# Ten weight slots of the adaptive conditioning move from beside the routers into the mixers, between products and heads

## The chip, the cores and the metric

One Trainium2 chip, one core. The metric is device time in microseconds for one execution of the whole program.

## The reference, cut to what matters

256 tokens of width 1024, float32, pass through two blocks. Block 1 is a mixer (16 attention heads of 64) followed by a mixture of 32 experts. Block 2 has two layers: a mixer of differential attention and a Fourier part with 16 experts behind it, then a short convolution with 16 experts behind it. In block 2 each layer l modulates its inputs by six vectors that come from a condition:

```python
def ada_params(cond, w_ada, b_ada):
    m = jax.nn.silu(cond) @ w_ada + b_ada
    return jnp.split(m[..., None, :], 6, axis=-1)

def modulate(x, g, shift, scale):
    return rmsnorm_2(x, g) * (1 + scale) + shift

def even_mixer(h, hc, w_in, q_norm, k_norm, lam, subln, w_out, lam_init, cos, sin, ctx_out):
    ...
    q, k, v, f = jnp.split(h @ w_in, cuts, axis=-1)
    q = apply_rope(rmsnorm_2(qk_heads(q), q_norm), cos, sin) * scale
    k = apply_rope(rmsnorm_2(qk_heads(k), k_norm), cos, sin)
    ...
```

In each layer the vectors 0 and 1 shift and scale the mixer's input, 2 gates its output, 3 and 4 shift and scale the experts' input, 5 gates their output.

## The kernel before, in words

**Phases.** The program runs mixer1, moe1, mixer2, moe2(0), mixer3, moe2(1), one behind the other. Each expert phase begins with its router (scores, a mask, positions, the gathering products `xg`) and goes on with one expert after the other (`gu`, then `d`).

**The weight stream.** All large weights come in tiles of 2 MB, 128 partitions by 4096 floats, in one fixed list that `plan` writes down. `Stream` puts each tile into a slot of a ring: six of its own, and up to three rooms (X, Y, Z) that are lent to it in stretches where nothing else needs them. Slots are reused in the order in which they were filled, and only when the kernel has called `done` for the tile that is in them. The loads (line 236) are all issued by SyncE's queue in the order of the list, and each issue waits for the last reader of the slot, so that one issue that waits holds up all behind it.

**The adaptive units.** There are twelve, named (l, v). `ada_unit` (line 569) takes two weight tiles, its two slots. For each it runs 8 small matmuls `ada_ps` (the trace counts 16), copies the result from PSUM into a row on ScalarE, and calls `done`. Then 8 transposes `adaT_ps` turn the row into columns, and VectorE reduces them.

**Where the units stand before.** (0,0) and (0,1) in mixer1; (0,3) and (0,2) in moe1's router, as fills between its steps; (0,4) at the start of mixer2; (1,0) and (1,1) between mixer2's products by way of `merged`, one slot behind each product; (0,5) and (1,2) in the router of moe2(0); (1,3) and (1,4) in mixer3; (1,5) in the router of moe2(1).

**Mixer2's products.** Five products of the normed input with 512 columns each, named by their first column (768, 0, 512, 1280, 1792), have eight k-steps: a weight tile's slice is split into a high part `wh` on ScalarE (line 338) and a low part `wl` on VectorE (line 339), and TensorE runs four matmuls with `wh` and two with `wl` (the function `three`). Behind the first four products `post` norms the heads and turns them (rope): `hss` on VectorE, `rs_r` on GpSimd, `xn` and `ro` on VectorE and GpSimd, for one half of the tokens and then the other; at last the transposes `qk_ps` (line 1328) on TensorE. The first two products have 8 heads of queries or keys, the next two 4, the last none. `chain` advances a product, the transposes of the one before, the norm, and then the fill. The compiler's scheduler may move independent instructions past each other, so the order on an engine is read from the built program.

**Mixer1's end.** `flow` interleaves the attention of eight pairs of heads (`duo`) with four output products (`out`), which read the tiles `out1`.

Of the kernel before, what the change touches and what calls it, by code (L numbers as in the profile page):

```python
# [10 lines left out]
F32 = mybir.dt.float32  # L11
I32 = mybir.dt.int32
F32R = mybir.dt.float32r
# [140 lines left out]
def chain(units, fill=iter(()), last=iter(())):  # L154
# [11 lines left out]
        last = finish  # L166
    for _ in last:
        pass


def merged(a, b):

    next(a)
    yield
    next(a)
    yield
    next(a, None)
    next(b)
    yield
    next(b)  # L180
    yield
    next(b, None)
    yield


def row_of(*units):
# [63 lines left out]
class Net:  # L250
# [180 lines left out]
    def plan(self):  # L431
        I, add = self.I, self.st.add

        def ada(l, v, hfs=(0, 1)):
            src = I["ada_w_2"][l].rearrange("(p k) f -> p k f", k=8)
            for hf in hfs:
                f0 = v * 1024 + hf * 512
                add(("ada", l, v, hf), src[:, :, f0:f0 + 512])

        def out(name, w):  # L440
            w = w.rearrange("(k p) d -> p k d", p=128)
            for i in range(2):
                add((name, i), w[:, 4 * i:4 * i + 4, :])

        win = I["w_in"][0].rearrange("(p k) f -> p k f", k=8)

        def in1(col):
            w = win[:, :, col:col + 512]
            add(("in1", col), *((w[:, 0:4], w[:, 4:8]) if col == 512 else (w,)))

        in1(512)
        in1(0)
        ada(0, 0, (0,))
        in1(1024)
        ada(0, 0, (1,))
        in1(2048)
        ada(0, 1, (0,))
        in1(1536)
        ada(0, 1, (1,))
        in1(2560)  # L460
        out("out1", I["w_out"][0])
        ada(0, 3)
        ada(0, 2)
        win2 = I["attn_w_in_2"][0].rearrange("(p k) f -> p k f", k=8)
        for e in range(32):
            add(("g", 0, e), I["w_gate"][0, e].rearrange("(p k) f -> p k f", k=8))
            add(("u", 0, e), I["w_up"][0, e].rearrange("(p k) f -> p k f", k=8))
            add(("d", 0, e), I["w_down"][0, e].rearrange("(n p c) d -> p n c d", n=2, c=2))
            i = CTX.index(e) // 2 - 1 if e in CTX and CTX.index(e) % 2 == 0 else -1
            if i >= 0:  # L470
                add(("ctx", i), win2[:, :, 768 + 512 * i:1280 + 512 * i])
        ada(0, 4)
        for i, c0 in enumerate((768, 0, 512, 1280, 1792)):
            if c0 == 512:
                add(("in2", 512), win2[:, :, 512:768], win2[:, :, 2304:2560])
            else:
                add(("in2", c0), win2[:, :, c0:c0 + 512])
            if i < 4:
                ada(1, i // 2, (i % 2,))
        out("out2", I["attn_w_out_2"][0])  # L480
        ada(0, 5)
        ada(1, 2)
        self.plan_moe2(0)
        win3 = I["conv_w_in_2"][0].rearrange("(p k) f -> p k f", k=8)
        for q in range(2):
            for n in (1, 2, 0):
                f0 = n * 1024 + q * 512
                add(("in3", n, q), win3[:, :, f0:f0 + 512])
            ada(1, 3 + q)
        out("out3", I["conv_w_out_2"][0])  # L490
        ada(1, 5)
        self.plan_moe2(1)

    def plan_moe2(self, l):
# [151 lines left out]
    def mixer1(self):  # L646
        nc, tc, I = self.nc, self.tc, self.I
        with ExitStack() as cx:
# [251 lines left out]
            self.lend("X", ("g", 0, CTX[0]))  # L900
            w = self.P("wr1", "p (k e) -> p k e", k=8)
            nc.gpsimd.tensor_tensor(w, w, self.P("g_ffn")[:, :, None].to_broadcast([128, 8, 64]), op=ALU.mult)
            flow([duo(4, 2), out(0, 0, 1), duo(5, 2), duo(6, 2), out(0, 1, 1), duo(7, 2), out(1, 0, 1, 1)])
            for _ in out(1, 1, 4):
                pass

# [171 lines left out]
    def moe1(self):  # L1078
        nc, tc, sm = self.nc, self.tc, self.sm
        with ExitStack() as cx:  # L1080
# [8 lines left out]
            for c in range(2):  # L1089
                nc.vector.scalar_tensor_tensor(zz[:, c, :], z[:, c, 0:36], r[:, c:c + 1], self.kp[:, a:a + 36], op0=ALU.mult,  # L1090
                                               op1=ALU.add)
            ze, zg = zz[:, :, 0:32], zz[:, :, 32:36]

            fills = [self.ada_unit(0, v, wk, ps, "a", "a", 3, 0, 3, wk.tile([128, 1024], F32, tag="row", name="row", bufs=2))
                     for v in (3, 2)]
            for i in (0, 0, 1):
                next(fills[i])
            mg = sm.tile([128, 2], F32, name="mg")
            nc.vector.tensor_reduce(out=mg, in_=zg, axis=AX.X, op=ALU.max)
            ohg = self.first_hot(wk, zg, mg, 4, "g")  # L1100
# [14 lines left out]
            mask = wk.tile([128, 2, 32], BF16, name="mask", bufs=1)  # L1115
            nc.vector.tensor_tensor(mask, oh1, oh2, op=ALU.add)
            pos = self.prefix(ps, mask, 32)
            next(fills[1])
            nc.vector.tensor_tensor(m2, m2, m1, op=ALU.subtract)
            nc.scalar.activation(m2, m2, AF.Exp)  # L1120
            g1 = sm.tile([128, 2], F32, name="g1")
# [18 lines left out]
                        (lambda n, c, j: wd[:, 2 * n + c, j * 256:j * 256 + 256]), done)  # L1140

            def first():
                for f in fills:
                    next(f, None)

                self.over = sm.tile([128, 2, 32], F32, name="over", bufs=1)
                nc.vector.tensor_scalar(self.over, pos[:, 0:2, :], 31.5, None, op0=ALU.is_ge)
                nc.vector.tensor_tensor(self.over, self.over, comb, op=ALU.mult)
                most = sm.tile([128, 1], F32, name="most", bufs=1)
                nc.vector.tensor_reduce(out=most, in_=pos[:, 2, :], axis=AX.X, op=ALU.max)  # L1150
                self.most = sm.tile([128, 1], I32, name="most_i", bufs=1)
                nc.vector.tensor_copy(self.most, most)
# [128 lines left out]
    def mixer2(self):  # L1281
        nc, tc, I, sm = self.nc, self.tc, self.I, self.sm
        with ExitStack() as cx:
# [116 lines left out]


            room, lows = [], {}
            high = self.cp.tile([128, 2, 8, 128], F32R, tag="xh", name="high")
            part = lambda k, c: (high[:, c, k, :], lows[k // 4][c][:, k % 4, :])

            def f_at(c):
# [2 lines left out]
            def sums():  # L1409
                fs = wk.tile([128, 2, 256], F32, tag="ro", name="fs", bufs=2)  # L1410
                for s, op in enumerate((ALU.add, ALU.subtract)):
                    nc.vector.tensor_tensor(fs[:, s, :], f_at(0), f_at(1), op=op)
                return fs

            tabs = self.roomy[:, 3072:3584]
            nc.gpsimd.dma_start(tabs, I["k_c"])
            chain([pair(768, 8, 1, 0), pair(0, 8, 0, 0), pair(512, 4, 0, 4, f_at),
                   pair(1280, 4, 1, 4, lambda c: v[:, c, 0:256]),
                   pair(1792, 0, 0, 0, lambda c: v[:, c, 256:768])],
                  merged(*(self.ada_unit(1, i, wk, ps, "pj", "tp", 4, 0, 2, q2[:, 2048:3072]) for i in range(2))))  # L1420
            fs = sums()
            t = self.room("X").rearrange("p (i b) -> p i b", b=512)
            room.extend((t[:, 0:4], t[:, 4:8]))
# [33 lines left out]
    def mixer3(self):  # L1457
        nc, tc = self.nc, self.tc
        with ExitStack() as cx:
# [11 lines left out]
            for q in range(2):  # L1471
# [22 lines left out]
                if q:  # L1494
                    self.lend("X")
                st.done(*[("in3", n, q) for n in (1, 2, 0)])
                for _ in self.ada_unit(1, 3 + q, wk, ps, "pj", "tp", 5, 0, 2, row):
                    pass
            self.router_bias(1, wk, "cv_a", 2, ps, "tp", 2)
            w = [st.take(("out3", i), 4) for i in range(2)]  # L1500
            for hf in range(2):
# [8 lines left out]
    def moe2(self, l):  # L1510
        nc, tc, sm = self.nc, self.tc, self.sm
        with ExitStack() as cx:
# [7 lines left out]
            aff = wk.tile([128, 2, 16], F32, name="aff", bufs=1)  # L1520
            for c in range(2):
                nc.vector.scalar_tensor_tensor(aff[:, c, :], z[:, c, 0:16], r[:, c:c + 1], self.rbias, op0=ALU.mult, op1=ALU.add)

            def unit(*u):
                row = wk.tile([128, 1024], F32, tag="row", name="row", bufs=2)
                return self.ada_unit(*u, wk, ps, "a", "a", 3, 0, 3, row)

            fill, also = unit(l, 5), iter(()) if l else unit(1, 2)
            next(fill)
            mx = sm.tile([128, 2], F32, name="ec_m")  # L1530
            nc.vector.tensor_reduce(out=mx, in_=aff, axis=AX.X, op=ALU.max)
            nc.vector.tensor_tensor(aff, aff, mx[:, :, None].to_broadcast([128, 2, 16]), op=ALU.subtract)
# [4 lines left out]
            b = ps.tile([16, 2, 128], F32, tag="a", name="affT_ps", bufs=3)  # L1537
            for c in range(2):
                nc.tensor.transpose(b[:, c, :], aff[:, c, :], self.ident)
            next(fill)  # L1540
            next(also, None)
            aT = wk.tile([16, 256], F32, tag="WT", name="affT")
            bT = b.rearrange("p c t -> p (c t)")
            m8 = None
# [14 lines left out]
            nc.vector.tensor_tensor(ge[:, :, 0:16], aff, tb, op=ALU.is_gt)  # L1559
            nc.vector.tensor_tensor(ge[:, :, 16:32], aff, tb, op=ALU.is_equal)  # L1560
            pre = self.prefix(ps, ge, 32)
            next(also, None)
            need = wk.tile([128, 16], F32, name="need", bufs=1)
            nc.vector.tensor_scalar(need, pre[:, 2, 0:16], -1.0, 32.0, op0=ALU.mult, op1=ALU.add)
            nb = need[:, None, :].to_broadcast([128, 2, 16])
# [21 lines left out]
            gate = wk.tile([128, 256], F32, name="gate", bufs=1)  # L1587

            def first():
                next(fill, None)  # L1590
                next(also, None)
                self.gate_quarters(l, 5, gate, wk, ps, "a", 3)

            def hook(e):
# [54 lines left out]
```

## Time and profile before

| | us |
|---|---|
| median of 3 runs | 1912.75 (1911.39 to 1913.34) |
| the profiled execution, its own time | 1912.47 |
| its span, first to last instruction | 1910.4 |
| outside the span | 2.1 |

The granted TensorE clock is 0.862 of full speed as a mean over the span. The profiled execution is 0.28 us below the median, so sums made on it apply to the median as they are. TensorE is busy for 71% of the span, VectorE 26%, ScalarE 19%, GpSimd 8%. Of the time of the 16 DMA engines 89.5% goes to the one queue that SyncE feeds.

### The profile page before, as it was taken

What the parts mean: (1) busy time and instruction counts of PE and PEld (TensorE: products, weight loads), DVE (VectorE), ACT (ScalarE), POOL (GpSimd) and SP (SyncE); (2) the same over time, 40 slices, a digit from 0 to 9 for tenths busy, and PEclk for the clock granted to TensorE, in tenths of its full rate; (3) what the DMA queues carried; (4) which work ended last, traced back from release to release, by engine and by line L of the source; (5) the groups of instructions that cost most, each with busy time, mean ns of one, the idle gap of its engine ahead of it and who ended that gap; (6) DMA issues with size and microseconds to landing.
All of it is one profiled execution on the core that took longest, in us unless ns stands there. A gap on an engine that the chain in (4) does not pass through costs nothing.

```text
span 1910.4 us, 27412 instructions
## 1 busy us (share of the span) xinstructions
PE 1363.1 (71%) x11863; PEld 756.5 (40%) x11863; DVE 492.5 (26%) x1189; ACT 361.1 (19%) x786; POOL 158.1 (8%) x217
## 2 busy tenths in 40 slices
PE   6989866667778678998565574565997664654745
PEld 4766533344444346564221221222984231221312
DVE  3666311121111056753010110102664110101101
ACT  4545100010111043742000000001442000000000
POOL 3132000010000034111000000001001000000000
PEclk9999988889999889989787787877998877877868
DMA  9645999999999997248999999999758999999998
GB/s 368 221 173 211 425 428 429 428 428 396 386 421 426 427 406 258 77 176 374 430 430 431 431 430 431 429 431 417 298 227 371 430 431 430 431 430 430 431 430 340
DMA packets 97691, 716.15 MB, mean 375 GB/s; under 512 B 5664, under 2 KB 7840, under 8 KB 56480
## 3 DMA queue, kind: packets, MB, share of 16 engines
q1 hardware_dynamic: 96960, 712.72, 89.5%
q8 instruction: 94, 1.54, 0.3%
q0 software_dynamic: 464, 1.57, 0.2%
q14 instruction: 29, 0.24, 0.0%
q10 hardware_dynamic: 144, 0.08, 0.0%
HBM read 713.30 MB, written 1.05 MB: 374 GB/s over the span
## 4 chain that ended last, share of the span: by engine, by line
DMA 39%; PE 31%; DVE 3%; POOL 2%; ACT 1%; issue 1%; SPq 0%; DVEq 0%; POOLq 0%; ACTq 0%
DMA w<-in_moe_w_up 18%; DMA w<-in_moe_w_gate 12%; PE gu_ps L997 9%; DMA w<-in_moe_w_down 7%; PE cv_ps L364 4%; PE pj_ps L364 3%; PE d_ps L1026 3%; DMA w<-in_w_up 2%; PE cx_ps L1261 2%; PE xg_ps L983 1%; PE sc_ps L1344 1%; PE o_ps L364 1%; PE ada_ps L580 1%; POOL rs_r L299 1%; PE y L1038 1%
## 5 line engine op out<-in xcount | busy, mean ns | idle before, releaser
L997 PE MATMUL gu_ps<-w,xgT 128*32 128x256 f32 (+1 forms) x4096 | 434.8, 586 | 302.4 <-DMA w<-in_moe_w_up 249.3
L997 PEld LDWEIGHTS gu_ps<-w,xgT 128*32 128x32 f32 x4096 | 146.4, 129 | 568.7 <-issue 262.9
L1005 DVE TENSOR_TENSOR h<-gu_ps,hs 64x256 f32<-64x256 f32 (+1 forms) x64 | 46.6, 727 | 778.0 <-ACT hs L1004 778.0
L1026 PE MATMUL d_ps<-w,eh 128*32 128x256 f32 x3072 | 203.1, 414 | 18.1 <-DMA w<-in_moe_w_down 7.2
L1004 ACT ACTIVATE hs<-gu_ps 64x256 f32<-64x256 f32 (+1 forms) x64 | 31.1, 487 | 921.7 <-PE gu_ps L997 921.7
L1026 PEld LDWEIGHTS d_ps<-w,eh 128*32 128x32 f32 x3072 | 97.2, 119 | 103.3 <-issue 30.4
L364 PE MATMUL pj_ps<-wh,roomX 128*128 128x512 f32 x352 | 106.4, 422 | 6.1 <-DVE xn L391 5.1
L339 DVE TENSOR_TENSOR wl<-w,wh 128x512 fp32r<-128x512 f32 x136 | 95.2, 712 | 41.9 <-ACT wh L338 36.5
L338 ACT ACTIVATE wh<-w 128x512 fp32r<-128x512 f32 x136 | 84.5, 630 | 90.3 <-PE cv_ps L364 36.7
L1018 PE MATMUL t_ps<-kp,h 64*128 64x64 f32 x192 | 25.3, 239 | 86.4 <-DVE h L1005 80.2
L364 PEld LDWEIGHTS pj_ps<-wh,roomX 128*128 128x128 f32 x352 | 69.6, 202 | 29.4 <-issue 6.7
L364 PE MATMUL cv_ps<-roomX,wh 128*128 128x256 f32 x384 | 71.9, 289 | 3.8 <-ACT wh L338 3.8
L983 PE MATMUL xg_ps<-Sg,xh 128*128 128x128 f32 x512 | 68.9, 293 | 2.3 <-DVE Sg L976 1.7
L983 PEld LDWEIGHTS xg_ps<-Sg,xh 128*128 128x128 f32 x512 | 63.8, 204 | 12.5 <-issue 10.8
L364 PE MATMUL pj_ps<-wl,roomX 128*128 128x512 f32 x176 | 59.4, 418 | 12.3 <-DVE wl L351 6.8
L1018 PEld LDWEIGHTS t_ps<-kp,h 64*128 64x128 f32 x192 | 16.6, 138 | 127.7 <-DVE h L1005 116.4
L364 PEld LDWEIGHTS cv_ps<-roomX,wh 128*128 128x128 f32 x384 | 61.9, 197 | 5.0 <-ACT wh L338 4.2
L364 PE MATMUL cv_ps<-roomX,wl 128*128 128x256 f32 x192 | 55.5, 289 | 0.2 <-DVE wl L339 0.2
L580 PE MATMUL ada_ps<-w,sc 128*32 128x512 f32 x384 | 48.9, 617 | 2.3 <-DVE x L271 2.2
L1038 PE MATMUL z<-ysb,WT 32*128 32x256 f32 x512 | 36.7, 400 | 16.9 <-DVE ysb L1033 16.9
L299 POOL TENSOR_TENSOR rs_r<-rs_r,mhalf 128x1 f32<-128x1 f32 (+3 forms) x45 | 44.9, 997 | 3.8
L1261 PE MATMUL cx_ps<-w,roomX 128*128 128x512 f32 x96 | 43.6, 602 | 0.0
(394 smaller groups left out, 1451.3 us busy)
## 6 DMA issues: line engine op xcount, KB each, us to landing
w<-in_moe_w_gate SPq DMA_DIRECT2D x64, 2048.0 KB, 38.5
w<-in_moe_w_up SPq DMA_DIRECT2D x64, 2048.0 KB, 28.8
w<-in_moe_w_down SPq DMA_DIRECT2D x63, 2048.0 KB, 32.7
w<-in_w_gate SPq DMA_DIRECT2D x32, 2048.0 KB, 20.3
w<-in_w_up SPq DMA_DIRECT2D x32, 2048.0 KB, 22.7
w<-in_w_down SPq DMA_DIRECT2D x32, 2048.0 KB, 23.5
w<-in_ada_w SPq DMA_DIRECT2D x24, 2048.0 KB, 11.9
w<-in_attn_w_in SPq DMA_DIRECT2D x7, 2048.0 KB, 14.6
```

The source lines that it names most:

```text
L299: nc.gpsimd.tensor_tensor(r, r, self.mhalf.to_broadcast(shape), op=ALU.pow)
L338: return (self.nc.scalar.activation(hi, src, AF.Copy), self.nc.vector.tensor_tensor(lo, src, hi.bitcast(F32), op=ALU.subtract))
L339: self.nc.vector.tensor_tensor(lo, src, hi.bitcast(F32), op=ALU.subtract))
L364: self.nc.tensor.matmul(o, l[a], r[b], start=first and n == 0, stop=last and n == 2)
L580: nc.tensor.matmul(b[32 * j:32 * j + 32, :], self.sc[:, 4 * kk + j, :], w[:, 4 * kk + j, :], start=kk == 0, stop=kk == 1)
L983: nc.tensor.matmul(b[:, k, :], self.xh[:, c, 2 * kq + k, :], Sg[:, c].rearrange("p e s -> p (e s)"), start=c == 0, stop=c == 1)
L997: nc.tensor.matmul(gu[32 * j:32 * j + 32, :], xgT[:, k, sl:sl + 32], w[:, n * Fh:n * Fh + Fh], start=k == 0, stop=k == 7)
L1005: nc.vector.tensor_tensor(h, gu[0:64, :].rearrange("p (m c) -> p c m", c=nch), hs.rearrange("p (m c) -> p c m", c=nch), op=ALU.mult)
L1018: nc.tensor.transpose(ht[:, c * 64:c * 64 + 64], h[:, c, :], self.ident[0:64, 0:64])
L1026: nc.tensor.matmul(d[32 * j:32 * j + 32, :], hT[:, c, n * 32:n * 32 + 32], wd(n, c, j), start=i == 0, stop=i == 2 * nch - 1)
L1038: nc.tensor.matmul(y[j][:, c, :], WT[r, c * 128:c * 128 + 128], ysb[r, :], start=e == 0 and c == 0, stop=e == ne - 1, skip_group_check=True)
L1261: nc.tensor.matmul(b, xr["hT"][:, k, c * 128:c * 128 + 128], w[:, k, :], start=k == 0, stop=k == 7)
```

## The change

Ten slots, that is five units, change place; the work in each and the sum of all transfers stay.

- (0,2) and (0,3) leave moe1's router and stand in mixer1's last `flow`, one behind `duo(5)`, one behind the second half of the first output group. Their order in the plan is swapped.
- `merged` goes. In mixer2 the new `fills` runs a whole unit, two slots, behind each of the first four products: (1,0), (1,1), (0,5), (1,2). The transposes of a unit come with the next fill. The rows lie in two halves of `xh`, so `high`, which has the same buffer, is allocated behind the products.
- (0,5) and (1,2) leave the router of moe2(0). (1,5) leaves the router of moe2(1) and stands in mixer3 directly behind (1,4), ahead of the output product.
- The plan follows: each of mixer2's first four input tiles has two adaptive tiles behind it, the experts' tiles of moe2(0) stand directly behind `out2`, and (1,5) stands ahead of `out3`.

```diff
-def merged(a, b):
-    next(a)
-    yield
...
@@ plan
+        ada(0, 2)
         ada(0, 3)
-        ada(0, 2)
...
             if i < 4:
-                ada(1, i // 2, (i % 2,))
+                ada(*((1, 0), (1, 1), (0, 5), (1, 2))[i])
         out("out2", I["attn_w_out_2"][0])
-        ada(0, 5)
-        ada(1, 2)
         self.plan_moe2(0)
...
+        ada(1, 5)
         out("out3", I["conv_w_out_2"][0])
-        ada(1, 5)
         self.plan_moe2(1)
@@ mixer1
-            flow([duo(4, 2), out(0, 0, 1), duo(5, 2), duo(6, 2), out(0, 1, 1), duo(7, 2), out(1, 0, 1, 1)])
+            flow([duo(4, 2), out(0, 0, 1), duo(5, 2), ada(2, row), duo(6, 2), out(0, 1, 1), ada(3, row), duo(7, 2), out(1, 0, 1, 1)])
@@ moe1, router
-            fills = [self.ada_unit(0, v, wk, ps, "a", "a", 3, 0, 3, wk.tile([128, 1024], F32, tag="row", name="row", bufs=2))
-                     for v in (3, 2)]
-            for i in (0, 0, 1):
-                next(fills[i])
...
@@ mixer2
+            def fills():
+
+                u = iter(())
+                for i, lv in enumerate(((1, 0), (1, 1), (0, 5), (1, 2))):
+                    next(u, None)
+                    u = self.ada_unit(*lv, wk, ps, "pj", "tp", 4, 0, 2, self.xh[:, i % 2].rearrange("p k m -> p (k m)"))
+                    next(u)
+                    next(u)
+                    yield
+                next(u, None)
+                yield
...
-                  merged(*(self.ada_unit(1, i, wk, ps, "pj", "tp", 4, 0, 2, q2[:, 2048:3072]) for i in range(2))))
+                  fills())
+            high = self.cp.tile([128, 2, 8, 128], F32R, tag="xh", name="high")
@@ mixer3
-                for _ in self.ada_unit(1, 3 + q, wk, ps, "pj", "tp", 5, 0, 2, row):
-                    pass
+                for v in ((4, 5) if q else (3,)):
+                    for _ in self.ada_unit(1, v, wk, ps, "pj", "tp", 5, 0, 2, row):
+                        pass
@@ moe2, router
-            fill, also = unit(l, 5), iter(()) if l else unit(1, 2)
-            next(fill)
...
```

What this does to the order on the engines is shown at three places. The first is TensorE near the end of mixer1, in the built program of before (`pj_ps` is an output product, `sc_ps`, `pT_ps` and `av_ps` are the attention):

```order
L803 MATMUL sc_ps<-dkT,dqT 128x128 x2
L824 MATMUL pT_ps<-kp,s 128x128 x6
L364 MATMUL pj_ps<-wh,oTf 128x512 x4
L364 MATMUL pj_ps<-wl,oTf 128x512 x2
L803 MATMUL sc_ps<-dkT,dqT 128x256 x2
L803 MATMUL sc_ps<-dkT,dqT 128x128 x2
L832 MATMUL av_ps<-pT,xh 64x256 x2
```

The same place in the changed program:

```order
L786 MATMUL sc_ps<-dkT,dqT 128x128 x2
L807 MATMUL pT_ps<-kp,s 128x128 x6
L349 MATMUL pj_ps<-wh,oTf 128x512 x4
L349 MATMUL pj_ps<-wl,oTf 128x512 x2
L563 MATMUL ada_ps<-w,sc 32x512 x8
L815 MATMUL av_ps<-pT,xh 64x256 x2
L817 MATMUL av_ps<-pT,xh 64x128 x2
```

One slot of (0,2) stands between an output product's step and the attention. There are four such groups of eight and two groups of eight transposes `adaT_ps` from here to the end of mixer1.

The second place is TensorE in mixer2, before, from the end of the first product (768) into the second:

```order
L364 MATMUL pj_ps<-wl,roomX 128x512 x2
L580 MATMUL ada_ps<-w,sc 32x512 x8
L364 MATMUL pj_ps<-wh,roomX 128x512 x4
L364 MATMUL pj_ps<-wl,roomX 128x512 x2
L364 MATMUL pj_ps<-wh,roomX 128x512 x4
L364 MATMUL pj_ps<-wl,roomX 128x512 x2
L364 MATMUL pj_ps<-wh,roomX 128x512 x4
L1328 MATMUL qk_ps<-kp,xn 128x128 x4
L364 MATMUL pj_ps<-wl,roomX 128x512 x2
```

The rest of the second product follows, and the other four `qk_ps` stand at its end. In the changed program the same place reads:

```order
L349 MATMUL pj_ps<-wl,roomX 128x512 x2
L563 MATMUL ada_ps<-w,sc 32x512 x16
L1303 MATMUL qk_ps<-kp,xn 128x128 x8
L575 MATMUL adaT_ps<-kp,xh 128x128 x6
L349 MATMUL pj_ps<-wh,roomX 128x512 x4
L349 MATMUL pj_ps<-wl,roomX 128x512 x2
```

Both slots of the unit and all eight head transposes of the product now stand ahead of the next product's first matmul. Behind the second, third and fourth product it is the same (eight `qk_ps`, then twice four).

The third place is ScalarE at the same point of mixer2 (`ro` is the square for the norm, `qT` the old row of the unit). Before:

```order
L382 ACTIVATE ro<-pj_ps 128x512
L338 ACTIVATE wh<-w 128x512 x2
L269 ACTIVATE qT_5124<-ada_ps 128x512
L382 ACTIVATE ro<-pj_ps 128x512
L338 ACTIVATE wh<-w 128x512 x3
L269 ACTIVATE roomY<-qk_ps 128x4x128
L338 ACTIVATE wh<-w 128x512 x3
```

And in the changed program:

```order
L367 ACTIVATE ro<-pj_ps 128x512
L254 ACTIVATE xh<-ada_ps 128x512
L367 ACTIVATE ro<-pj_ps 128x512
L254 ACTIVATE xh<-ada_ps 128x512
L254 ACTIVATE roomY<-qk_ps 128x4x128
L323 ACTIVATE wh<-w 128x512 x8
```

All eight high parts for the next product now stand behind the copy of the first product's heads.

## Rows read from the trace of the kernel before

**Rows 1.** The page: DMA share in 40 slices, and the chain that ended last.

```profile
DMA  9645999999999997248999999999758999999998
...
DMA 39%; PE 31%; DVE 3%; POOL 2%; ACT 1%; issue 1%; SPq 0%; DVEq 0%; POOLq 0%; ACTq 0%
```

**Rows 2.** Windows: from:to, length, busy per engine, clock, DMA share, GB/s.

```profile
140.00:176.00 36.00, 35.32 (x202) 27.29 (x203) 27.54 (x92) 20.87 (x61) 3.01 (x4) 1.00 0.42 159
176.00:690.00 514.00, 381.75 (x4306) 210.73 (x4305) 92.55 (x280) 66.20 (x168) 37.12 (x45) 0.90 1.00 418
...
780.00:838.00 58.00, 56.79 (x237) 32.42 (x238) 35.27 (x90) 40.12 (x110) 9.63 (x23) 0.85 0.00 1
...
869.00:1330.00 461.00, 280.50 (x2627) 114.18 (x2628) 56.13 (x136) 31.19 (x61) 7.53 (x11) 0.80 1.01 428
```

**Rows 3.** Timeline of SyncE's issues around moe1's start: start, us, instruction.

```profile
99.05 38.02 SPq L236 DMA_DIRECT2D w<-in_ada_w  x4
...
176.32 0.38 SPq L236 DMA_DIRECT2D w<-in_w_down  x1
...
177.78 0.33 SPq L236 DMA_DIRECT2D w<-in_w_up  x1
190.51 0.38 SPq L236 DMA_DIRECT2D w<-in_w_down  x1
```

**Rows 4.** Timeline of TensorE in moe1's router.

```profile
194.64 1.92 PE L580 MATMUL ada_ps<-w,sc 128*32 128x512 f32 x16
```

**Rows 5.** Timeline of TensorE in mixer2; in brackets idle before, releaser.

```profile
702.51 1.92 PE L580 MATMUL ada_ps<-w,sc 128*32 128x512 f32 x16
...
733.07 1.22 PE L364 MATMUL pj_ps<-wl,roomX 128*128 128x512 f32 x2 [2.45 <-DVE wl L339]
734.09 1.91 PE L364 MATMUL pj_ps<-wh,roomX 128*128 128x512 f32 x4
...
746.33 1.19 PE L364 MATMUL pj_ps<-wh,roomX 128*128 128x512 f32 x4
...
757.40 0.60 PE L1328 MATMUL qk_ps<-kp,xn 128*128 128x128 f32 x4
...
772.75 0.60 PE L1328 MATMUL qk_ps<-kp,xn 128*128 128x128 f32 x4
...
774.97 0.71 PE L592 MATMUL adaT_ps<-kp,qT 128*128 128x128 f32 x4 [0.33 <-DVE roomY L271]
```

**Rows 6.** Timelines of GpSimd and VectorE in mixer2: the norm and rope.

```profile
709.91 0.75 POOL L298 TENSOR_SCALAR rs_r<-hss 128x8 f32<-128x8 f32 x1
...
714.80 1.60 POOL L409 TENSOR_TENSOR xn<-xn,roomZ 128x512 f32<-128x512 f32 x1 [0.29 <-DVE ro L407]
...
766.02 0.77 POOL L409 TENSOR_TENSOR xn<-xn,roomZ 128x256 f32<-128x256 f32 x1 [0.25 <-DVE ro L407]
...
716.88 0.68 DVE L410 TENSOR_TENSOR xn<-xn,ro 128x512 f32<-128x512 f32 x1
```

**Rows 7.** Timeline of SyncE's issues from mixer2 into moe2(0).

```profile
746.45 23.92 SPq L236 DMA_DIRECT2D w<-in_ada_w  x4
...
854.86 14.41 SPq L236 DMA_DIRECT2D w<-in_moe_w_down  x2
...
876.17 7.67 SPq L236 DMA_DIRECT2D w<-in_moe_w_up  x2
```

**Rows 8.** Timeline of TensorE in the routers of moe2(0) and moe2(1).

```profile
876.04 3.84 PE L983 MATMUL xg_ps<-Sg,xh 128*128 128x128 f32 x32
...
1461.90 6.06 PE L983 MATMUL xg_ps<-Sg,xh 128*128 128x128 f32 x32 [1.72 <-DVE Sg L976]
```

**Rows 9.** Timelines of TensorE in mixer3 and of SyncE into moe2(1).

```profile
1415.12 3.64 PE L580 MATMUL ada_ps<-w,sc 128*32 128x512 f32 x32
...
1419.72 1.05 PE L592 MATMUL adaT_ps<-kp,xh 128*128 128x128 f32 x8
...
1457.24 14.65 SPq L236 DMA_DIRECT2D w<-in_moe_w_up  x2
```

More of the change, by code (lines that the diff above doesn't have):

```diff
@@ L168, in chain @@
         pass
-def merged(a, b):
-    next(a)
-    yield
[L175 to L183, printed above, removed]
 def row_of(*units):
@@ L1117, in moe1 @@
             pos = self.prefix(ps, mask, 32)
-            next(fills[1])
             nc.vector.tensor_tensor(m2, m2, m1, op=ALU.subtract)
@@ L1142, in first @@
             def first():
-                for f in fills:
-                    next(f, None)
                 self.over = sm.tile([128, 2, 32], F32, name="over", bufs=1)
@@ L1402, in mixer2 @@
             room, lows = [], {}
-            high = self.cp.tile([128, 2, 8, 128], F32R, tag="xh", name="high")
             part = lambda k, c: (high[:, c, k, :], lows[k // 4][c][:, k % 4, :])
@@ L1522, in moe2 @@
                 nc.vector.scalar_tensor_tensor(aff[:, c, :], z[:, c, 0:16], r[:, c:c + 1], self.rbias, op0=ALU.mult, op1=ALU.add)
-            def unit(*u):
-                row = wk.tile([128, 1024], F32, tag="row", name="row", bufs=2)
-                return self.ada_unit(*u, wk, ps, "a", "a", 3, 0, 3, row)
-            fill, also = unit(l, 5), iter(()) if l else unit(1, 2)
-            next(fill)
             mx = sm.tile([128, 2], F32, name="ec_m")
@@ L1539, in moe2 @@
                 nc.tensor.transpose(b[:, c, :], aff[:, c, :], self.ident)
-            next(fill)
-            next(also, None)
             aT = wk.tile([16, 256], F32, tag="WT", name="affT")
@@ L1561, in moe2 @@
             pre = self.prefix(ps, ge, 32)
-            next(also, None)
             need = wk.tile([128, 16], F32, name="need", bufs=1)
@@ L1589, in first @@
             def first():
-                next(fill, None)
-                next(also, None)
                 self.gate_quarters(l, 5, gate, wk, ps, "a", 3)
```

## The prediction, made before the changed kernel was run

> **What bounds the kernel now.** I read the page first: its line of DMA shares says which phases wait for weights, and the chain that ended last gives transfers 39% and TensorE 31% of the span [rows 1]. So there are two kinds of phase, and the windows show where each lies. In the expert phases the DMA share is 1.00 to 1.01 and 418 to 428 GB/s move, while TensorE is busy for 382 of 514 and 281 of 461 us: the weights decide. In the mixers it is the other way round: in 140 to 176 us TensorE is busy for 35.32 of 36.00 us at a DMA share of 0.42, and in 780 to 838 for 56.79 of 58.00 at a share of 0.00 [rows 2]. Next I read SyncE's issues at each change from a mixer to its experts, since what holds an issue there says when the stream of weights starts, and at last TensorE, VectorE and GpSimd one instruction at a time in mixer2.
>
> A tile has 128 x 4096 floats, 2.097 MB; at 428 GB/s [rows 2] that is 4.90 us. Ten slots are 49.0 us of transfers. The question for each of the three places is what of that leaves a phase in which weights decide, and what the work costs where TensorE decides.
>
> **Mixer1 and moe1 (four slots).** The four tiles concerned are issued at 99.05 and within the 38.02 us behind it, so they are loaded beside mixer1 already; the change only frees them earlier. The stream into the experts becomes continuous at 176.32, where a down tile is issued once the last output product has released its slot; the next one that waits for an adaptive slot, at 190.51, comes 14.19 us later, which is less than the three tiles issued from 176.32 to 177.78 take (3 x 4.90 = 14.7) [rows 3]. Slots are reused in order, so freed adaptive slots stand behind that output tile. No transfer is gained: 0. The cost is TensorE's: a slot takes 1.92 us [rows 4], the transposes of a unit 1.05 [rows 9]. Four slots and two sets are 4 x 1.92 + 2 x 1.05 = 9.8 us in front of the release at 176.32. Cover would be TensorE's idle time there, which is 0.68 us in all [rows 2]. Bounds: 9.1 with that used up, and 14 if each of the six insertions also waits 0.7 us for a copy, between the 0.33 and 2.45 of [rows 5]. I take 9.8, the row's own price, and as the clock is 1.00 there [rows 2]. Behind it the whole program comes later by that much. In moe1's router the removed work stood in waits for VectorE, so I give it back nothing.
>
> **Mixer2 (four slots more than before; all the order of the products).** Before, from the end of the first product at 702.51 to the end of the last at 772.75, 70.24 us pass [rows 5] with four products, the transposes and four slots. That is tight because the next product's steps fill the time in which the heads are normed. How long that takes: the first half's work on GpSimd gives way to the second's at 709.91, the last multiplication there runs from 714.80 to 716.40, and VectorE's sum ends at 717.56 [rows 6], 15.05 us behind the product. For four heads GpSimd ends at 766.79 [rows 6], 9.39 us behind the end at 757.40 [rows 5]; with the sum on VectorE some 9.9, and up to 11.4 where VectorE is also busy with low parts; I take 10.5.
>
> In the changed order all transposes of a product's heads stand ahead of the next product, and so do the high parts on ScalarE. Then TensorE has 3.64 us for two slots [rows 9], and otherwise waits. A cycle becomes: norm, second half's transposes (0.60, [rows 5]), the copy and the unit's transposes beside each other (about 1.1), and an unbroken product of 11.07 us (746.33 to 757.40, [rows 5]). With 8 heads: 15.05 + 0.6 + 1.1 + 11.07 = 27.8; with 4 heads: 10.5 + 0.5 + 1.1 + 11.07 = 23.2. Twice each makes 102.0 us, 31.8 more than 70.24. The two groups of adaptive transposes that stood behind the last product go, 0.71 us and a wait of 0.33 for the second [rows 5], about 1.3 with both. So +30.5. Bounds: +26 with 14.5 and 9.5 for the two norms, if low parts no longer cut in; +36 if copies to the new rows, in ScalarE's queue between the two squares, delay the second half by 1.5 us in each cycle.
>
> **TensorE's clock in these stalls.** Each of the cycles with 8 heads has two idle stretches: from the slots' end, 3.64 us behind the product, until the first half is done soon after GpSimd's 7.4 (709.91 - 702.51, [rows 5, 6]), and from there until 15; with 4 heads they are shorter. Behind 2.45 us of idle time one step took 1.22 and 1.91 us where the same groups take about 0.7 and 1.19 elsewhere [rows 5], so a stall can cost 1.2 us of slow matmuls. Four cycles: +5, from 0 (another step behind such a wait shows none) to 9. The Trainium skill says of this, in "TensorE: Matmul & The Clock Gate" under "What's actually happening", that the throttled state is the default and activity releases it; the row agrees, in that the granted speed of 2.4 GHz was lost behind idle time. By that rule alone each product would begin at 1.2 GHz, which is the fourth rival below.
>
> **What moe2(0) gets back.** Before, the four tiles of (0,5) and (1,2) are issued at 746.45 and within 23.92 us, and hold four slots until the router is done. The stream is continuous from the second down tile, at 854.86 + 14.41 - 0.3 = 868.95, onwards [rows 7]. In the changed plan these four slots can be refilled with experts' tiles in 780 to 838, where the DMA share is 0.00 [rows 2]. That fills the ring with nine of the phase's tiles; the tenth, the fourth up tile, needs a slot that only the first expert's gate and up products release, as its issue at 876.17 + 7.67 - 0.3 = 883.5 shows [rows 7]. So it lands at 883.5 + 4.9, and before at 868.95 + 5 x 4.90 = 893.4, both with the same start-up time: 5.0 us gained, not four tiles' 19.6. From there on the phase waits for weights as before.
>
> The router itself gains nothing, since the slots filled waits for VectorE; but without them TensorE is idle. In moe2(0), where slots filled the waits, `xg` took 3.84 us; in moe2(1), behind idle time, 6.06 [rows 8]. I charge 2.2 us for that to moe2(0), whose first products now set the stream; from 0 to 3.
>
> **Mixer3 and moe2(1) (two slots).** Mixer3's unit takes 3.64 us for two slots and 1.05 for its transposes [rows 9]; a second directly behind it, which has to wait for the shared row between, is 3.64 + 1.05 + 0.7 = 5.4 us on TensorE. Back comes nothing: in moe2(1) the fourth up tile was issued at 1457.24 + 14.65 - 0.3 = 1471.6 [rows 9], at the release by the first products, so it is that which sets the stream there already. Some more idle time in the router: +0.7 (0 to 2).
>
> **The sum.** 1912.5 + 9.8 + 30.5 + 5 - 5.0 + 2.2 + 5.4 + 0.7 = 1961.1. The profiled execution is within 0.3 us of the median, so I forecast **1961 us**. With the bounds of the terms its own range is 1946 to 1975.
>
> **The rivals.**
> - **The ten transfers are gained (faster).** If the experts really waited for each of the ten slots, 49.0 us of transfers move to stretches in which the DMA engines are idle. Against it TensorE gets 9.8 us in mixer1, four more slots and two sets of transposes (9.8) in mixer2 and 5.4 in mixer3: 1912.5 - 49.0 + 25.0 = 1888. It decides if the ring can run ahead by more tiles than its nine slots, or the first gate and up products come early. For it speaks the DMA share of 0.00 in 780 to 838 [rows 2]; against it that the stream begins with a release by TensorE at all three places. Chance 0.08. The Trainium skill's "Perfetto Trace Analysis", under "Optimization Strategy", says that where a kernel has several regimes with different contended engines, interleaving them may improve it; the rows show the regimes, and here the ring's size would keep most of it from paying.
> - **Plain insertion.** The wait for the heads is hidden after all, and mixer2 pays only the 9.8 us of matmuls: 1912.5 + 9.8 + 9.8 - 5.0 + 5.4 = 1932.5. It needs TensorE to find the transposes' input ready 4 us behind a product; the norm takes 15 [rows 5, 6]. Chance 0.12.
> - **No change to be measured.** The insertions take the place of waits everywhere; 0.68 us of idle time in mixer1 [rows 2] excludes it there. 1912 to 1916, chance 0.03.
> - **The clock stays low.** Every product behind a stall runs half its length at 1.2 GHz: 4 x 11.07 / 2 = 22 us in place of 5: 1978. The row for it is the 1.91 us step, against it the next step is fast again [rows 5]. Chance 0.10.
>
> **How the numbers follow.** My forecast has 0.67, insertion 0.12, the low clock 0.10, the gained transfers 0.08, no change 0.03. Below 1932 lie 0.11, above 1975 about 0.06, so the range is 1932 to 1975. Within 0.2%, 3.8 us, a measurement of this kernel can't tell a change. Slower by more: 0.67 + 0.12 + 0.10 = 0.89; same 0.03; faster 0.08.
>
> **What would show it.** In the changed profile: the down tile that was issued at 176.32 comes about 10 us later, with a continuous stream behind it; TensorE in mixer2 waits twice behind each of four products, for `xn` from VectorE, and the stretch from the first to the last product's end is about 102 us and some for the clock; nine experts' tiles of moe2(0) are issued without a gap between them that waits for the router; mixer3 grows by 5 us; moe2(1) keeps its length. I am wrong if the products in mixer2 follow each other as before, or if moe1 or moe2(0) becomes shorter by more than a tile or two.

## The result

The changed kernel takes 1936.61 us (median of 4 runs, 1935.8 to 1937.64) against 1912.22 us before: ratio 1.0127, 95% interval 1.011 to 1.0145, 24.4 us slower. The forecast was 48.6 us slower, with the same sign and twice the size. The profiled execution has a span of 1935.7 us, 25.3 more than before; the mean granted TensorE clock is 0.860. Five points that are in both traces, and the end, say where these lie:

| up to | before | after | shift | added here | the prediction's terms |
|---|---|---|---|---|---|
| end of mixer2's first product | 702.51 | 703.78 | +1.3 | +1.3 | +9.8 |
| end of its last product | 772.75 | 804.83 | +32.1 | +30.8 | +30.5 + 5 |
| first `gu` of moe2(0) | 879.81 | 905.54 | +25.7 | -6.4 | +2.2 |
| first product of mixer3 | 1338.44 | 1357.29 | +18.9 | -6.9 | -5.0 |
| first `gu` of moe2(1) | 1467.90 | 1490.86 | +23.0 | +4.1 | +5.4 + 0.7 |
| the end of the span | 1910.4 | 1935.7 | +25.3 | +2.3 | 0 |

The large term is there, at 30.8 of 35.5. Two of the others are not: mixer1 costs nearly nothing, and behind the products time comes back.

**After, SyncE's issues around moe1's start** (the timeline), and two of before that [rows 3] leave out:

```profile
147.82 0.35 SPq L221 DMA_DIRECT2D w<-in_w_up  x1
155.16 0.38 SPq L221 DMA_DIRECT2D w<-in_w_down  x1
160.81 0.33 SPq L221 DMA_DIRECT2D w<-in_w_gate  x1
163.91 0.33 SPq L221 DMA_DIRECT2D w<-in_w_up  x1
168.64 0.38 SPq L221 DMA_DIRECT2D w<-in_w_down  x1
...
184.74 0.38 SPq L221 DMA_DIRECT2D w<-in_w_down  x1
210.13 0.33 SPq L221 DMA_DIRECT2D w<-in_w_gate  x1
```

```profile
161.06 0.35 SPq L236 DMA_DIRECT2D w<-in_w_up  x1
...
203.99 0.33 SPq L236 DMA_DIRECT2D w<-in_w_gate  x1
```

**After, TensorE there** (the timeline):

```profile
145.84 1.92 PE L563 MATMUL ada_ps<-w,sc 128*32 128x512 f32 x16
...
153.18 1.92 PE L563 MATMUL ada_ps<-w,sc 128*32 128x512 f32 x16
...
199.06 0.21 PE L1049 MATMUL pre_ps<-mask,cnt 128*128 128x32 bf16 x1 [5.92 <-DVE mask L1094]
...
200.28 6.19 PE L966 MATMUL xg_ps<-Sg,xh 128*128 128x128 f32 x32 [0.91 <-DVE over L1122]
206.41 3.66 PE L980 MATMUL gu_ps<-w,xgT 128*32 128x256 f32 x64
```

The first slot's matmuls end at 145.84 + 1.92 = 147.76, and the up tile that waited until 161.06 before is issued at 147.82; the second's end at 155.10, and the down tile that waited until 176.32 goes at 155.16. So a freed adaptive slot is refilled at once; an output tile's slot follows in between, at 163.91, when VectorE's last split of that tile is done (163.88). By 184.74 all nine tiles that the ring holds are issued, and the next one waits for the first `gu` until 210.13: now TensorE's first products, not an output tile, set the stream.

**Windows of moe1's router**, before and then after (length, busy PE, PEld, DVE, ACT, POOL, clock, DMA share, GB/s):

```profile
178.00:204.00 26.00, 22.88 (x222) 13.05 (x223) 11.96 (x51) 8.41 (x19) 9.32 (x7) 0.93 1.01 427
```

```profile
186.00:210.00 24.00, 15.62 (x158) 11.96 (x158) 11.77 (x49) 4.11 (x11) 9.30 (x7) 0.79 0.56 239
```

Before, transfers run without a gap up to the first `gu`, and the tile issued at 203.99 queues behind others. After, the nine tiles have landed before the first `gu` is done, and the DMA engines stand nearly idle until it is (share 0.02 from 200 to 205).

**After, TensorE in mixer2** (the timeline; [rows 5]): the first cycle with 8 heads, the first with 4, and the end of the last product.

```profile
703.78 3.64 PE L563 MATMUL ada_ps<-w,sc 128*32 128x512 f32 x32
711.10 1.09 PE L1303 MATMUL qk_ps<-kp,xn 128*128 128x128 f32 x4 [3.68 <-DVE xn L395]
716.85 1.09 PE L1303 MATMUL qk_ps<-kp,xn 128*128 128x128 f32 x4 [4.66 <-DVE xn L395]
...
719.07 1.92 PE L349 MATMUL pj_ps<-wh,roomX 128*128 128x512 f32 x4
...
758.48 3.64 PE L563 MATMUL ada_ps<-w,sc 128*32 128x512 f32 x32
763.16 0.41 PE L1303 MATMUL qk_ps<-kp,xn 128*128 128x128 f32 x2 [1.04 <-DVE xn L395]
766.83 0.66 PE L1303 MATMUL qk_ps<-kp,xn 128*128 128x128 f32 x2 [3.26 <-DVE xn L395]
...
804.83 1.95 PE L1363 MATMUL ft_ps<-roomY,fs 128*128 128x128 f32 x16
```

TensorE waits twice behind each product for `xn`, as forecast. The norm of 8 heads is ready 13.1 us behind the product (the estimate was 15.05), that of 4 heads 8.4 (10.5), and the next product's first step runs slowly, 1.92 us in place of 1.07 to 1.19.

**After, windows of mixer2's heads and output product**, and then of the kernel before the stretch in which its clock falls (columns as above):

```profile
805.00:838.00 33.00, 31.77 (x134) 16.65 (x134) 23.15 (x57) 27.28 (x71) 6.32 (x12) 1.00 0.10 40
838.00:883.00 45.00, 41.51 (x213) 29.75 (x213) 28.35 (x61) 26.46 (x69) 7.30 (x15) 1.00 0.47 193
```

```profile
814.00:831.00 17.00, 17.00 (x45) 9.78 (x45) 7.84 (x19) 8.25 (x22) 1.58 (x4) 0.52 0.00 0
```

Before, the granted clock fell to 0.52 for 17 us in the attention heads, 41 to 58 us behind the last product, with TensorE busy throughout. The same distance behind the last product lies at 846 to 863 after, and the clock is 1.00 there. From the last product to the end of the output product the kernel before takes 85.4 us and the changed one 75.9, which is 9.5 less: half of 17 us is 8.5, and the adaptive transposes that stood there are gone. The router takes 3.1 more (24.9 against 21.7), so 6.4 us come back.

**After, from mixer2 into moe2(0), and the two units of mixer3** (timelines of SyncE and TensorE; [rows 7 to 9]), and the first `gu` of moe2(0) before:

```profile
861.15 0.80 SPq L221 DMA_DIRECT2D w<-in_moe_w_down  x2
863.70 11.27 SPq L221 DMA_DIRECT2D w<-in_moe_w_gate  x2
877.44 32.10 SPq L221 DMA_DIRECT2D w<-in_moe_w_up  x2
...
898.87 6.74 PE L966 MATMUL xg_ps<-Sg,xh 128*128 128x128 f32 x32 [1.72 <-DVE Sg L959]
905.54 7.07 PE L980 MATMUL gu_ps<-w,xgT 128*32 128x512 f32 x64
...
1433.88 4.48 PE L563 MATMUL ada_ps<-w,sc 128*32 128x512 f32 x34
1438.29 1.16 PE L575 MATMUL adaT_ps<-kp,xh 128*128 128x128 f32 x8
1439.38 3.63 PE L563 MATMUL ada_ps<-w,sc 128*32 128x512 f32 x30
...
1485.70 5.24 PE L966 MATMUL xg_ps<-Sg,xh 128*128 128x128 f32 x32 [1.72 <-DVE Sg L959]
```

```profile
879.81 7.07 PE L997 MATMUL gu_ps<-w,xgT 128*32 128x512 f32 x64
```

The second up tile of that pair, the tenth of the phase, is issued at 877.44 + 32.10 - 0.33 = 909.2, when half of the first `gu` is done: the ring gives back one tile, as the prediction said, and no more.

### The profile page after: what moved, and what is told of

The parts are those of the page before. It is cut to its first block, busy times and chain, and to the rows that moved or that the text cites. A ratio compares the mean times of both kernels' runs of the same rounds, so it can differ in the third digit from the quotient of the medians.

```text
span 1935.7 us, 27434 instructions
## 1 busy us (share of the span) xinstructions
PE 1349.9 (70%) x11863; PEld 754.8 (39%) x11863; DVE 490.7 (25%) x1189; ACT 360.5 (19%) x786; POOL 153.6 (8%) x217
## 4 chain that ended last, share of the span: by engine, by line
DMA 40%; PE 29%; DVE 3%; POOL 3%; ACT 1%; issue 1%; SPq 0%; DVEq 0%; POOLq 0%; ACTq 0%
DMA w<-in_moe_w_up 18%; DMA w<-in_moe_w_gate 14%; PE gu_ps L980 9%; DMA w<-in_moe_w_down 5%; PE pj_ps L349 4%; DMA w<-in_w_up 4%; PE cv_ps L349 4%; PE d_ps L1009 2%; PE cx_ps L1236 1%; PE xg_ps L966 1%; PE o_ps L349 1%; POOL rs_r L284 1%; PE sc_ps L1319 1%; PE ada_ps L563 1%; PE y L1021 1%
## 5 line engine op out<-in xcount | busy, mean ns | idle before, releaser
L980 PE MATMUL gu_ps<-w,xgT 128*32 128x256 f32 (+1 forms) x4096 | 430.2, 576 | 303.5 <-DMA w<-in_moe_w_up 250.3
## 6 DMA issues: line engine op xcount, KB each, us to landing
w<-in_w_down SPq DMA_DIRECT2D x32, 2048.0 KB, 21.7
```

Of the source, the lines that this page charges most:

```text
L980: nc.tensor.matmul(gu[32 * j:32 * j + 32, :], xgT[:, k, sl:sl + 32], w[:, n * Fh:n * Fh + Fh], start=k == 0, stop=k == 7)
```

## The experiments

Medians; the ratio is to runs of the kernel before on the same chip (their medians: 1910.56 for e1 to e4, 1910.5 for e5 to e8, 1910.86 for e9 and e10). `held` keeps an instruction in the program's order on its engine.

### The change in its three parts

Each is the kernel before with one part of the diff and its lines of the plan, nothing else.

**e1**, mixer1 alone:

```diff
+        ada(0, 2)
         ada(0, 3)
-        ada(0, 2)
...
-            flow([duo(4, 2), out(0, 0, 1), duo(5, 2), duo(6, 2), out(0, 1, 1), duo(7, 2), out(1, 0, 1, 1)])
+            flow([duo(4, 2), out(0, 0, 1), duo(5, 2), ada(2, row), duo(6, 2), out(0, 1, 1), ada(3, row), duo(7, 2), out(1, 0, 1, 1)])
```

> Only (0,2) and (0,3) move, from moe1's router into mixer1. The prediction's term says 9.8 us slower (1922), since slots are reused in order and no transfer is gained. The rival, from the trace of the changed kernel: the freed adaptive slots are refilled at once, the up, down and gate tiles of the first experts are issued from about 148 us on, the ring is then full with nine tiles and waits for the first gate and up products near 210, so that cost and gain cancel: within 2 us of before. The gathering products in the router run near 6.2 us in place of 3.84.

Measured: 1911.32 us, 1.001 (0.9996 to 1.0024): no change. Its stream has the early issues of the changed kernel, the ring full from 186.23, and the next gate tile at 211.95.

**e2**, mixer2 and moe2(0) alone:

```diff
-                  merged(*(self.ada_unit(1, i, wk, ps, "pj", "tp", 4, 0, 2, q2[:, 2048:3072]) for i in range(2))))
+                  fills())
```

> Only the part on mixer2 and moe2(0): two slots behind each of four products, none in that router. The prediction's terms give 30.5 + 5 + 2.2 - 5.0 = 33 us slower (1945). From the changed trace: products' stretch 70.2 to 101 us (+31), attention heads behind it about 9.5 shorter because the clock does not fall there, router 3 longer, ring 5 back: 19 to 20 slower (1932). If the heads run at the lower clock as before, 28 to 29 slower (1941).

Measured: 1929.58 us, 1.0107 (1.0079 to 1.0136), 19.0 slower. The products run from 702.59 to 803.64, 101.05 us; the clock in the heads and the output product is 1.00 from 804 to 882.

**e3**, mixer3 alone:

```diff
-                for _ in self.ada_unit(1, 3 + q, wk, ps, "pj", "tp", 5, 0, 2, row):
-                    pass
+                for v in ((4, 5) if q else (3,)):
+                    for _ in self.ada_unit(1, v, wk, ps, "pj", "tp", 5, 0, 2, row):
+                        pass
```

> Only (1,5) moves, from the router of moe2(1) into mixer3. The prediction's terms: 5.4 + 0.7 = 6.1 us slower (1918.5). From the changed trace: 2.7 us up to the fourth up tile and 2.5 in the last expert, together about 5 (1917.5). The rival that the transfers are gained: 9.8 us faster less 5.4, 1908.

Measured: 1916.57 us, 1.0035 (1.0019 to 1.0051), 6.0 slower: the prediction's 6.1, and near the 5 read from the trace, though its eleven runs lie between 1907.8 and 1920.44. No transfer is gained. The three parts add to 25.8 us, the whole change to 24.4.

### What holds mixer2's products

**e4**, the changed kernel with the heads' transposes pinned behind the next product:

```diff
-                        nc.tensor.transpose(t[:, j, :], xf[:, j * 128:j * 128 + 128], self.ident)
+                        self.held(nc.tensor.transpose(t[:, j, :], xf[:, j * 128:j * 128 + 128], self.ident))
```

> The changed kernel, with the transposes of the heads pinned behind the next product on TensorE; the orders on VectorE and ScalarE are left to the scheduler, and it still puts the low parts of the next product behind the whole norm. If TensorE's order makes the stall, as the prediction has it, the products' stretch falls from 101 to about 80 us and the kernel gets 20 us faster than the changed one (1917). The rival: the low parts on VectorE, or the two PSUM banks of the fill, hold the next product just as long; then TensorE waits for VectorE behind the first step, and only the transposes' own wait goes: stretch 92 to 98 us, 3 to 9 us faster (1928 to 1934).

Measured: 1937.37 us (five runs, 1928.69 to 1939.99), 1.0153 (1.0124 to 1.0182): as slow as the changed kernel. In the profiled execution, the fastest of the five, the products' stretch is 91 us and TensorE waits elsewhere (timeline):

```profile
706.35 1.21 PE L349 MATMUL pj_ps<-wh,roomX 128*128 128x512 f32 x4 [1.29 <-ACT wh L323]
715.02 1.22 PE L349 MATMUL pj_ps<-wl,roomX 128*128 128x512 f32 x2 [7.46 <-DVE wl L324]
```

One step with the high parts runs, and then the low part on VectorE, which stands behind the whole norm in that engine's order, holds it for 7.46 us. The rival is right for this execution: TensorE's order alone is not it. Why the other four runs gave the 10 us of stretch back can't be read; their mean clock was 0.857 to 0.859, that of the profiled one 0.863.

**e10**, the changed kernel with the fill in two other PSUM banks:

```diff
-                    u = self.ada_unit(*lv, wk, ps, "pj", "tp", 4, 0, 2, self.xh[:, i % 2].rearrange("p k m -> p (k m)"))
+                    u = self.ada_unit(*lv, wk, ps, "av", "tp", 2, 0, 2, self.xh[:, i % 2].rearrange("p k m -> p (k m)"))
```

> The changed kernel with the fills in two other PSUM banks and nothing else; the scheduler gives TensorE the same order as in the changed kernel. If the order holds the products, nothing changes (1935 to 1938, stretch 101). If it were the two banks that the fill takes from the next product, the stretch falls by some 8 us and the kernel by as much (1929).

Measured: 1935.72 us, 1.0129 (1.0115 to 1.0144): nothing changes. The banks alone don't hold the products.

**e5**, the changed kernel with both orders undone, in the banks of e10 (the norm is cut into four pieces, each pinned on its engines):

```diff
+            def woven(units, fill):
+                last = iter(())
+                for product, finish in units:
+                    for k in range(8):
+                        next(product, None)
+                        if k in (0, 2, 5):
+                            next(last, None)
+                    next(product, None)
+                    for _ in last:
+                        pass
+                    next(finish, None)
+                    next(fill, None)
+                    last = finish
...
-            chain([pair(768, 8, 1, 0), pair(0, 8, 0, 0), pair(512, 4, 0, 4, f_at),
+            woven([pair(768, 8, 1, 0), pair(0, 8, 0, 0), pair(512, 4, 0, 4, f_at),
```

> The changed kernel with both orders undone: the norm of the heads is written in pieces between the next product's steps and pinned there on VectorE, GpSimd and TensorE, and the fills take two other PSUM banks. If the order makes the stall, TensorE goes from a product through the fill into the next with no wait of more than some 2 us, and the stretch of the products falls from 101 us to 68 to 75: 26 to 33 faster than the changed kernel, 1904 to 1911, or some 9 more if the clock falls in the attention heads as in the kernel before. The rival: the two adaptive tiles ahead of each input tile make it late, TensorE waits for transfers, and the stretch stays above 90 (1926 or more).

Measured: 1908.72 us, 1.0001 (0.9986 to 1.0017) to before, 28 us less than the changed kernel, or 24 by the two ratios, as the chips differ. TensorE (timeline; the last row shows the end of the last product):

```profile
701.23 3.64 PE L563 MATMUL ada_ps<-w,sc 128*32 128x512 f32 x32
706.17 1.19 PE L349 MATMUL pj_ps<-wh,roomX 128*128 128x512 f32 x4 [1.29 <-ACT wh L323]
...
718.25 1.03 PE L1341 MATMUL qk_ps<-kp,xn 128*128 128x128 f32 x8
...
775.79 0.60 PE L1341 MATMUL qk_ps<-kp,xn 128*128 128x128 f32 x4
```

The stretch is 74.6 us, the longest wait behind a product 1.3. No input tile comes late, so the two adaptive tiles ahead of each were no fault. So the stall of the changed kernel lies in the order that the scheduler gave to the engines that this run pins together: TensorE, VectorE, and parts of ScalarE's and GpSimd's share of the norm. TensorE's alone (e4) is not enough, nor are the banks (e10); which of the rest is needed was not run, nor the woven order in the old banks.

**e6**, the kernel before with the same woven order, no slot moved:

> The kernel before with the same woven order and the other PSUM banks, one slot behind each product as before; no slot moves. TensorE's short waits (1.48, 2.47, 1.31, 2.45, 1.01 us) go: stretch 70 to 60 to 64, 6 to 10 us faster than before (1901 to 1905) if the router behind it follows, unchanged if the clock takes it back. For the theory of the order: the order alone, without any move, is worth more than the move. For the rival that the move itself is at fault, no effect.

Measured: 1894.8 us, 0.9926 (0.9908 to 0.9945), 15.7 faster, more than expected. The stretch is 764.68 - 702.57 = 62.1 us in place of 70.2, and the clock in 814 to 831 is 1.00 in place of 0.52: the heads and the router behind it take 100.9 us and not 107.1. So about 8 us are the order's, and about 6 go with the clock; that the order holds the clock is not shown.

e5 and e6 have the same order, the same banks and the same chip, and differ only in the ten slots. So the move costs 1908.72 - 1894.8 = 13.9 us even where the order is held, 12.5 of it in the products (74.6 against 62.1; the prediction's price of the work alone was 9.8). Of the 30.8 us that the products lost, the order that came with the move has the other 18.

### Mixer1's slots and the routers

**e7**, the kernel before with half of e1, (0,2) alone in mixer1:

```diff
-            flow([duo(4, 2), out(0, 0, 1), duo(5, 2), duo(6, 2), out(0, 1, 1), duo(7, 2), out(1, 0, 1, 1)])
+            flow([duo(4, 2), out(0, 0, 1), duo(5, 2), ada(2, row), duo(6, 2), out(0, 1, 1), duo(7, 2), out(1, 0, 1, 1)])
```

> The kernel before with one unit, (0,2), in mixer1 and (0,3) left in the router, where it keeps TensorE busy. By the prediction's term 4.9 us slower (1915). By the account of e1 (early tiles gained, first products' release the limit): the release comes near 207 with the gathering products near 3.84 us, and the fourth gate tile is issued at it, so 2 to 4 us faster than before (1907 to 1909).

Measured: 1906.1 us, 0.9979 (0.9969 to 0.9989), 4.4 faster. TensorE's gathering products take 3.84 us and the fourth gate tile is issued at 206.06 (e1: 5.84 and 211.95). Mixer2's first product ends at 696.97 in place of 702.51, 5.5 us earlier, 1.3 of it since the loads began earlier (97.79 against 99.05): the rest is the gain, in moe1. Of 11 runs the profiled one was the fastest, so its later times prove little.

**e8**, the changed kernel with matmuls that nothing reads in the routers' waits (the output is not touched):

```diff
+    def warm(self, ps, n):
+        b = ps.tile([128, 512], F32, tag="a", name="warm_ps", bufs=3)
+        for m in range(n):
+            for j in range(4):
+                self.held(self.nc.tensor.matmul(b[32 * j:32 * j + 32, :], self.sc[:, j, :], self.x[:, m % 2, 0:512],
+                                                start=True, stop=True))
```

> The changed kernel with work added that nothing reads: 40 to 64 small matmuls (form of the adaptive ones, on data that is there) in the waits of each of the three routers. If the gathering products are slow because TensorE is idle before them, they return to about 3.84 us from 6.19, 6.74 and 5.24, and as the first release sets each stream, the kernel gets 5 to 7 us faster than the changed one (1930 to 1932). The rival: other things set the streams, or the added work delays the masks: no change or slower than 1936.

Measured: 1926.26 us, 1.0085 (1.0072 to 1.0099), 10 us faster than the changed kernel, or 8 by the two ratios. TensorE in moe1's and moe2(0)'s router (timeline):

```profile
201.39 1.07 PE L277 MATMUL warm_ps<-x,sc 128*32 128x512 f32 x8
202.38 3.84 PE L974 MATMUL xg_ps<-Sg,xh 128*128 128x128 f32 x32
...
892.18 1.92 PE L277 MATMUL warm_ps<-x,sc 128*32 128x512 f32 x16
894.03 3.84 PE L974 MATMUL xg_ps<-Sg,xh 128*128 128x128 f32 x32
```

So part of what the fills in the routers did before was to keep the clock up, and that is worth time where the first `gu` sets the stream. The three `xg` are 6.7 us shorter together, which doesn't make up the whole; where the rest comes from is not shown.

**e9**, e6, e7 and e8's matmuls in the router of moe2(1), together, on the kernel before:

> The kernel before with three things put together: the woven order in mixer2 (e6, 15.7 us), one unit (0,2) in mixer1 (e7, 4.4 us), and 16 matmuls that nothing reads in the waits of the router of moe2(1), so that its gathering products run near 3.84 us in place of 6.06 (about 2 us by e8's account). If the three act in different phases, they add up: 22 us faster than before, 1887 to 1891. The rival: the stages take from each other, and it stays near e6's 1895.

Measured: 1892.3 us, 0.9916 (0.9899 to 0.9933), 18.6 faster than before, the best here. It is 2.5 us below e6, and its interval overlaps e6's; that the parts add to the 22 expected is not shown; `xg` in moe2(1) did fall to 3.84.

## Why the prediction was half wrong, step by step

**Mixer1 and moe1: the step that failed.** "Slots are reused in order, so freed adaptive slots stand behind that output tile. No transfer is gained: 0." The row at 147.82, 0.06 us behind the slot's last matmul, shows the opposite, and e1 and e7 confirm it: tiles go into slots in the order in which the readers let them go, and not, as the description of the kernel before has it too, in the order in which they were filled. The down tile that was to come 10 us later than 176.32 came at 155.16. TensorE's cost was nearly right, 8.3 us of 9.8: mixer1's last product ends 7.0 later in the trace, which begins its loads 1.35 earlier. But up to four tiles are loaded meanwhile, and what sets the stream is no longer the output tile but the first `gu`, at 210.13 in place of 203.99 by the trace. Before, that release had slack, since transfers were queued ahead of it (DMA share 1.01 there, 0.56 after). In moe1's router `xg` rose too (3.84 to 6.19), which the prediction put at nothing, but the router lost its fills and is shorter in all, 21.7 us in place of 22.6. So the whole move is worth 0 (e1, 9.8 predicted), and half of it, which keeps fills in the router, is worth 4.4 us.

**Mixer2's order: the mechanism right, the size 4.7 too large.** 30.8 us against 30.5 and 5 for the clock: the norms were 2 us shorter each than the estimate, and the slow steps are inside the 30.8. e5 takes 26.5 us away by undoing the orders, of which 8.1 can be had without the move (e6). As the prediction had it, order is the larger part: TensorE's alone (e4) doesn't undo it, since VectorE's low parts stand behind the norm too; the prediction named the high parts on ScalarE and not the low parts.

**What comes behind the products: mis-sized, a thing not seen.** I charged 2.2 us for a slower router; it rose by 3.1, 2.90 of it in `xg` (3.84 to 6.74), so that was nearly right. What I had not read in the trace of before, and put at nothing, were 17 us at half the clock in the attention heads (0.52, its window above). They are gone after, and in e2, e5, e6 and e8 to e10. That gives -6.4 in place of +2.2.

**The ring: right.** 5.0 predicted, 6.9 measured up to mixer3, and the tenth tile at the first release. **Mixer3: right.** 6.1 predicted, 6.0 in e3; in the whole change 4.1 up to the first `gu` of moe2(1). The last expert's products, 10.03 us where before they took 8.72 (first rows of each below), and its `d` add 2.3 that no term had:

```profile
1909.35 10.03 PE L980 MATMUL gu_ps<-w,xgT 128*32 128x512 f32 x64 [11.13 <-DMA w<-in_moe_w_up]
```

```profile
1886.53 8.72 PE L997 MATMUL gu_ps<-w,xgT 128*32 128x512 f32 x64 [9.59 <-DMA w<-in_moe_w_up]
```

**The rivals.** The gained transfers, priced at 49 us, are real in mixer1 only, beside the ring's one, and cancel there. Plain insertion, 1932.5, is nearest in size, by accident: the stall it denies is there. The clock that stays low is refuted: at most two of a product's eight steps are slow, and the others take 1.07 or 1.08 us with the high parts as elsewhere. "No change" is excluded by the 24.4 us. The bounds of my terms add to 1948 and 1977, where I wrote 1946 and 1975; that the wider range holds the result is owed to the insertion rival, and is luck. The Trainium skill's rule in "TensorE: Matmul & The Clock Gate", "What's actually happening", that activity releases the throttle, agrees with e8 (6.19, 6.74 and 5.24 us of `xg` back to 3.84). It does not explain the window of before, where the clock fell with TensorE busy for 17.00 of 17.00 us.

**What stays open.** Why the clock falls in the heads of the kernel before, e1 and e3 (0.51 and 0.56 in the same 17 us) and not after. It isn't tied to one instruction or one length: in e4 it fell at other heads, from 803 to 813, and in e7 for 7 us only, from 809. Nor does each execution need to show it alike: the runs of the kernel before lie between 1901.28 us at a mean clock of 0.871 and 1913.49 at 0.863, and there is one trace of each kernel. So how much of the 6.4 us the change itself brings is not shown. No run was made for it.

## What to carry to other kernels

Before a transfer is called not gained, find in the trace which reader each refill followed, to the hundredth of a us, rather than deduce it from the list's order; and look at what sets the stream next, since a release with slack becomes the limit. Where work moves between two phases of a static schedule, read the order on every engine that feeds the one that waits: with a fill twice as long the scheduler put the norm ahead of the next product on VectorE and TensorE, and pinning an interleaved order gave more (15.7 us, some 6 of it with the clock) than any move. Then price the work itself too, for with the order held the move still cost 13.9 us. Removing fills from waits is not free: they held the clock (`xg` 3.84 us with them, 6.74 without).

## What the runs showed of the hardware that was not expected

The granted clock fell to half (0.51 to 0.56 over 17 us) in a stretch where TensorE was busy without a gap, in three traces, for some 10 and 7 us in two more (e4, e7), and stayed at 1.00 in the same heads of the seven others. By half of 17 us, an estimate, it makes some 8 us of the time of a kernel that runs at 1910, as much as most of the terms here.
